# Softmax attention: normalising three of four head pairs later, from sums kept in DRAM

## The chip, the cores and the metric

The kernel runs on one core of a Trainium2 chip. Times are device microseconds of the program on that core. The engines are PE (TensorE, with its weight loads PEld), DVE (VectorE), ACT (ScalarE), POOL (GpSimd) and SP (SyncE, which here only issues transfers). Each engine takes its own instructions in program order, and waits on semaphores for the others.

## The reference

A two-layer trunk over 1040 tokens (16 learned ones and 1024) of width 1024. In each layer a group of gated-linear-attention heads (GLA) and a group of eight softmax heads with a forget bias (FoX) share one input projection; their normalised outputs go through one output projection, and a gated feed-forward block with a convolution of width 3 follows. The change is in the FoX heads:

```python
log_f = jax.nn.log_sigmoid(ff + b_forget[i])          # c = cumsum(log_f)
logits = einsum('bqhd,bkhd->bhqk', q_b * dh**-0.5, k) + c_q[..., None] - c_k[:, :, None, :]
logits = where(key_pos <= q_pos, logits, -inf)
o_fox = einsum('bhqk,bkhd->bqhd', softmax(logits), v)  # 8 heads of 64
o_fox = rms_norm(o_fox, fox_norm[i])                   # over the 64 of each head
h = h + concatenate([o_gla, o_fox], -1) @ w_out[i]
```

Because the norm follows, the softmax denominator d need not be divided out: with O the unnormalised sum over keys, `rms_norm(O/d) = O * rsqrt(mean(O*O) + EPS*d*d)`.

## The kernel before, in words

Activations are held with channels on partitions and tokens along the free side. Every large product is made in three passes of a split into a high and a low part (`mm<-xh,hi`, `mm<-xh,lo`, `mm<-xl,hi`, lines 257 to 259). Weights arrive as `raw`, and ACT or POOL and DVE split them (`hi`, `lo`, lines 224 and 226). The eight FoX heads are four pairs, p = 0 to 3, of two heads e = 0, 1. Tokens form nine tiles of 116 (the first 112), taken in five groups: (7,8), (5,6), (3,4), (1,2), (0).

`fox` walks over slots, one per pair, group, head and tile: 18 slots a pair, 72 in all. In a slot n a tile's scores are made (PE `S`, lines 713 and 714; DVE adds the bias row `cb` and takes the running minimum, line 716; ACT makes the exponential `P`, line 728). Two slots later P is transposed (PE `tr` line 749, ACT and DVE split it into `PT`, lines 373 and 374), three slots later the product with V follows (`av`, line 775). The fold (`fox_fold`) comes four slots after the last tile of head 1, and the store (`fox_store`) six. V holds high and low parts side by side, so that `av` has them in two partition halves, which ACT copies to `avs` (line 778). The fold transposes `avs` back to tokens on partitions (`fo`, line 788; four transposes for a two-tile group, two for the one-tile group), adds the halves (`ff`), squares and sums them along the free side (`fon`, `fv`), adds the squared denominator `fd`, takes the inverse root of the four numbers per token (`rsqrt`, lines 308 to 312: a logarithm and an exponential on ACT, three small operations on DVE) and multiplies (line 803). The store transposes the result again (line 814), ACT scales it into `fst` (line 821), and POOL's queue writes it to `mixd[4 + p]` in DRAM (line 822). For pair 3 the result goes into the operand of the output projection directly.

Between these steps `work.run` fills PE with other products, whose amount is planned by `plan(p)`: the next pair's projections, the GLA gate `gr` (evacuated by DVE, lines 673 to 684), and from slot 8 of pair 3 on (slot 62) the output projection (`wo`), whose operand is read back from `mixd` (`h<-mixd`, lines 1024 and 1032, on POOL's queue) and split into `mh` and `ml`. The Python order hands the steps to a list scheduler, which sets the final order on each engine; the scores have a higher priority. POOL also adds the causal mask to the next tile's columns of `cb` (line 893), and SP issues the loads of weights, of keys (`kA`, `kL`) and of the bias rows.

PSUM banks of one tag, `S`, serve the scores, the fold's and the store's transposes.

Of the kernel before, what the change touches and what calls it, by code (L numbers as in the profile page):

```python
# [168 lines left out]
class Kern:  # L169
    def __init__(self, ctx, tc, hT0, wm, wd, vec, wau, out):  # L170
# [26 lines left out]
        self.cd = dp.tile([8, T], F32, name="cd")  # L197
        self.later = []
# [554 lines left out]
    def fox_av(self, e, tiles, q, PT, avs, pp, part):  # L753
# [23 lines left out]
        if last < 4 * part + 4:  # L777
            nc.scalar.copy(avs[:, e, :width], av[:, :width])

# [27 lines left out]
    def fox_store(self, lyr, p, tiles, on, ap, pp, mix):  # L807
# [9 lines left out]
        if mix is not None:  # L817
            self.split(mix[0][:, c0:c0 + n], mix[1][:, c0:c0 + n], trf[:, :n], self.v(lyr, V_XN, p))
            return
        st = ap.tile([128, 2 * FT], F32, tag="fst", name="fst", bufs=1)  # L820
        nc.scalar.mul(st[:, :n], trf[:, :n], self.v(lyr, V_XN, p))
        nc.gpsimd.dma_start(self.mixd[4 + p][:, c0:c0 + n], st[:, :n])

    def fox(self, lyr, ap, pp, qs, plan, mix3):
# [9 lines left out]
        cbs, state, due = {}, {}, {}  # L834
# [9 lines left out]
        for n in range(len(steps) + 8):  # L844
# [7 lines left out]
            for kind in ('av0', 'T0'):  # L852
                run(n, kind)
            if n < len(steps):
# [12 lines left out]
                if e == 0 and ti == len(tiles) - 1:  # L867
                    state[p, g] = {"den": ap.tile([128, 2, 2], F32, tag="den", name="den", bufs=3)}
# [3 lines left out]
                with self.tc.high_priority(8):  # L872
                    Ps = self.fox_scores(e, i, qs[p], cbs[p][e], st["den"][:rows, ti, e:e + 1], ap, pp)
                if i:
                    self.fox_mask(cbs[p][e], i - 1)
                self.fox_schedule(lyr, at, n, p, e, ti, i, tiles, Ps, st, qs[p], ap, pp, mix3)
# [3 lines left out]
            run(n, "fold")  # L880
            for c in parts:
                run(n, "av" + c)
                run(n, "T" + c)
                work.run(fill_us / (1 + len(parts)))
        work.drain()
# [9 lines left out]
    def fox_schedule(self, lyr, at, n, p, e, ti, i, tiles, Ps, st, q, ap, pp, mix3):  # L895
# [18 lines left out]
        def av(ci):  # L914
            def f():
                if e == 0 and ci == 0:
                    one = len(tiles) == 1
                    st["avs"] = ap.tile([128, 2, FT if one else 2 * FT], F32, tag="av1" if one else "avs",
                                        name="avs", bufs=1)
                self.fox_av(e, tiles, q, PT, st["avs"], pp, ci)  # L920
# [5 lines left out]
        def store():  # L926
            self.fox_store(lyr, p, tiles, st["on"], ap, pp, mix3() if p == 3 else None)
        for ci in range(PT["nch"]):
            at(n + 3, f"av{ci}", av(ci))
        if e == 1:  # L930
            at(n + 4, "fold", fold)
            at(n + 6, "store", store)

# [6 lines left out]
    def attention(self, lyr, nm, hsrc, chunks, feed):  # L940
        tc, nc, s = self.tc, self.nc, self.slots
        with tc.tile_pool(name=f"aps{lyr}", bufs=2, space=PSUM, reuse_waits="tile") as pp2, \
# [64 lines left out]
            with tc.tile_pool(name=f"att{lyr}", bufs=2, reuse_waits="tile") as ap, \  # L1007
                    tc.tile_pool(name=f"lent{lyr}", bufs=1, reuse_waits="tile") as lp:
                s.lent = s.add(lp, 2, f"a{lyr}_")
                box = {}  # L1010
                KORD = (4, 5, 0, 1, 2, 3, 6)
# [929 lines left out]
```

## Time and profile before

| | |
|---|---|
| time, median of 3 runs | 2474.95 us (2473.05 to 2475.42) |
| profiled execution | 2476.73 us, its span 2474.8 us |
| granted PE clock, mean | 0.996 |
| PE busy | 2443.6 us (99%) |
| DVE busy | 1874.5 us (76%) |
| ACT busy | 1319.5 us (53%) |
| POOL busy | 383.1 us (15%) |

The profiled execution is 1.8 us above the median. Its span is the time from the first to the last instruction; 1.9 us lie around it. FoX takes from about 172 to 490 us in layer 0. In the rows of groups, the two numbers behind the bar are the busy time of all together and the mean ns of one; after the second bar stands the engine's idle time just before, and what ended most of it. In a row of the timeline the first number is the start, the second the duration.

### The profile page before, as it was taken

How to read it: one execution, taken by the hardware profiler on the slowest of the kernel's cores; microseconds unless marked ns; L12 is line 12 of the kernel's file. 1: busy time of each engine (PE TensorE's matmuls, PEld its weight loads, DVE VectorE, ACT ScalarE, POOL GpSimd, SP SyncE). 2: the span in 40 equal slices, each digit the busy share in tenths (PEclk: the TensorE clock that was granted, in tenths of full speed). 3: DMA queues.
4: the chain of work that ended last, by engine and by line, in shares of the span. 5: the costliest groups of instructions: out<-in, count | busy, mean ns of one | idle time of the engine just before them, and what ended most of it. 6: DMA issues, size and time to landing. Idle time of an engine off the chain costs nothing.

```text
span 2474.8 us, 47318 instructions
## 1 busy us (share of the span) xinstructions
PE 2443.6 (99%) x18286; PEld 2361.8 (95%) x18286; DVE 1874.5 (76%) x3769; ACT 1319.5 (53%) x2857; POOL 383.1 (15%) x565
## 2 busy tenths in 40 slices
PE   9999999999999999999999999999999999999998
PEld 8999999999999999999999999999999999997887
DVE  7656776869988888855866666777699888887667
ACT  7345666636555555642543456666465555556433
POOL 2023333210000000100220234331100000001002
PEclk9999999999999999999999999999999999999999
DMA  4232134433322224764312222243433212247722
GB/s 135 74 84 74 41 98 126 129 120 108 113 77 86 82 74 144 185 161 139 125 43 74 80 78 69 72 141 108 147 85 114 91 65 90 85 146 184 211 71 87
DMA packets 121824, 260.91 MB, mean 105 GB/s; under 512 B 15136, under 2 KB 36896, under 8 KB 121600
## 3 DMA queue, kind: packets, MB, share of 16 engines
q1 hardware_dynamic: 97440, 182.78, 23.9%
q0 software_dynamic: 22288, 72.81, 10.5%
q8 instruction: 143, 2.34, 0.4%
q10 hardware_dynamic: 1872, 2.31, 0.3%
q14 instruction: 81, 0.66, 0.1%
HBM read 177.26 MB, written 67.80 MB: 99 GB/s over the span
## 4 chain that ended last, share of the span: by engine, by line
PE 50%; issue 31%; DVE 11%; ACT 4%; DMA 2%; POOL 1%; SPq 0%; DVEq 0%; POOLq 0%; ACTq 0%
PE mm L257 8%; PE mm L259 7%; PE mm L258 7%; PE down L258 4%; PE down L257 4%; PE down L259 4%; PE av L775 3%; PE tr L749 2%; PE S L713 1%; DVE S L716 1%; PE wo L259 1%; PE wo L257 1%; PE wo L258 1%; PE S L714 1%; DVE x L1182 1%
## 5 line engine op out<-in xcount | busy, mean ns | idle before, releaser
L258 PE MATMUL up<-x,lo 128*128 128x260 f32 x2240 | 631.8, 282 | 0.8 <-DVE lo L1157 0.8
L259 PE MATMUL up<-x,hi 128*128 128x260 f32 x2240 | 631.8, 282 | 0.0
L257 PE MATMUL up<-x,hi 128*128 128x260 f32 x2240 | 631.7, 282 | 0.0
L258 PEld LDWEIGHTS up<-x,lo 128*128 128x128 f32 x2240 | 421.8, 188 | 1.3 <-DVE lo L1157 1.2
L257 PEld LDWEIGHTS up<-x,hi 128*128 128x128 f32 x2240 | 421.8, 188 | 0.2
L259 PEld LDWEIGHTS up<-x,hi 128*128 128x128 f32 x2240 | 421.9, 188 | 0.0
L1156 ACT CAST hi<-raw 128x512 fp32r<-128x512 f32 (+1 forms) x490 | 266.4, 553 | 208.2 <-PE up L259 89.2
L257 PE MATMUL mm<-xh,hi 128*128 128x348 f32 (+5 forms) x1056 | 361.2, 342 | 0.0
L1157 DVE TENSOR_TENSOR lo<-raw,hi 128x512 fp32r<-128x512 f32 (+1 forms) x490 | 288.1, 603 | 80.6 <-ACT hi L1156 80.1
L259 PE MATMUL mm<-xl,hi 128*128 128x348 f32 (+5 forms) x1056 | 340.5, 322 | 0.0
L258 PE MATMUL mm<-xh,lo 128*128 128x348 f32 (+5 forms) x1056 | 339.8, 322 | 0.0
L257 PEld LDWEIGHTS mm<-xh,hi 128*128 128x128 f32 x1056 | 200.3, 190 | 2.2 <-issue 1.4
L258 PEld LDWEIGHTS mm<-xh,lo 128*128 128x128 f32 x1056 | 200.5, 190 | 0.2
L259 PEld LDWEIGHTS mm<-xl,hi 128*128 128x128 f32 x1056 | 199.5, 189 | 0.1
L1138 DVE TENSOR_TENSOR raw<-raw,raw 128x512 f32<-128x512 f32 (+1 forms) x230 | 147.6, 652 | 28.1 <-DMA raw<-in_wd_dram 25.7
L728 ACT ACTIVATE P<-S,m 116x460 f32<-116x460 f32 (+2 forms) x224 | 125.0, 562 | 77.0 <-DVE m L716 74.1
L258 PE MATMUL down<-x,lo 128*128 128x260 f32 (+1 forms) x504 | 161.2, 320 | 0.5 <-DVE lo L1157 0.5
L259 PE MATMUL down<-x,hi 128*128 128x260 f32 (+1 forms) x504 | 161.1, 320 | 0.0
L257 PE MATMUL down<-x,hi 128*128 128x260 f32 (+1 forms) x504 | 161.0, 320 | 0.0
L224 ACT CAST hi<-raw 128x512 fp32r<-128x512 f32 (+2 forms) x152 | 87.4, 576 | 138.0 <-PE mm L259 53.7
L374 DVE TENSOR_TENSOR PT<-tr,PT 116x464 fp32r<-116x464 f32 (+3 forms) x240 | 123.2, 516 | 48.8 <-ACT PT L373 47.2
L1418 POOL DMA_DIRECT2D actd<-cv x44 | 23.6, 535 | 735.1 <-DVE cv L1417 735.1
(313 smaller groups left out, 5960.3 us busy)
## 6 DMA issues: line engine op xcount, KB each, us to landing
raw<-in_wm_dram SPq DMA_DIRECT2D x330, 256.0 KB, 3.1
raw<-in_wd_dram SPq DMA_DIRECT2D x48, 256.0 KB, 4.3
actd<-cv POOLq DMA_DIRECT2D x22, 520.0 KB, 3.0
actd<-cv POOLq DMA_DIRECT2D x22, 512.0 KB, 3.0
cb<-cd SPq DMA_DIRECT2D x16, 520.0 KB, 4.0
kA<-kA SPq DMA_DIRECT2D x24, 260.0 KB, 4.2
kL<-kL SPq DMA_DIRECT2D x24, 260.0 KB, 4.8
st<-actd SPq DMA_DIRECT2D x24, 260.0 KB, 3.5
```

The costliest lines, as they stand in the source:

```text
L224: nc.scalar.copy(hi[:, :n, :], raw[:, :n, :])
L257: nc.tensor.matmul(ps, wh, xh[:, c0:c0 + n], start=first, stop=False, skip_group_check=more)
L258: nc.tensor.matmul(ps, wl, xh[:, c0:c0 + n], start=False, stop=False, skip_group_check=more)
L259: nc.tensor.matmul(ps, wh, xl[:, c0:c0 + n], start=False, stop=last, skip_group_check=more)
L374: nc.vector.tensor_tensor(out=lo, in0=src, in1=hi.bitcast(F32), op=ALU.subtract)
L713: nc.tensor.matmul(S[:rows, :n], q["qA"][e][:, qs], q["kA"][e][:, c0:k1], start=True, stop=False)
L728: nc.scalar.activation(P[:rows, :n], S[:rows, :n], AF.Exp, scale=-1.0, bias=m[:rows, nch - 1:nch], accum_out=(den if nch == 1 else d3[:row ...
L749: nc.tensor.transpose(tr[:w, 3 - j, :rows], P[:rows, o:o + w], id_)
L775: nc.tensor.matmul(av[:, a:b], w.rearrange("p a b -> p (a b)"), x, start=(t == ts[0] and part == 0 and i == 0), stop=(t == last and i == 1))
L1138: nc.vector.tensor_tensor(out=q[out][:, :nk, :], in0=q[a][:, :nk, :], in1=q[b][:, :nk, :], op=op)
L1156: nc.scalar.copy(hi[:, :nk, :], src[:, :nk, :])
L1157: nc.vector.tensor_tensor(out=lo[:, :nk, :], in0=src[:, :nk, :], in1=hi[:, :nk, :].bitcast(F32), op=ALU.subtract)
```

## The change

Pair 3 stays as it was. For pairs 0 to 2 there is no fold and no store:

- `fox_av` copies one half of `av` with ACT, and DVE adds the other half: the sum O of a head, 64 rows by up to 232 columns. Behind head 1, POOL's queue stores the 128 rows of O to `mixd[4 + p]`, unnormalised. For groups 0 to 2 this store is handed out a slot later.
- The denominators of a pair gather in one tile (`denp`). `fox_den` squares and scales them after groups 2 and 4, PE transposes them, ACT copies them, and SP stores them as rows to DRAM (`dd`, `de`).
- Later (at 12, 10, 8, 6 and 6 slots behind a group's last tile) SP loads O back (`fO`, two buffers by turns), ACT squares it, and ACT and DVE split the square (`fsh`, `fsl`). A slot on, SP spreads the denominators over 64 partitions of each head (`fd`). Another slot on, PE sums the squares over each head's 64 rows with a block matrix of ones (`pair`, two matmuls of 232 columns, in a bank of tag `S`), DVE adds the denominators, the inverse root is taken on 128 rows by 232 columns (two ACT, three DVE operations), and DVE multiplies O in place. POOL's queue stores it to the same place of `mixd` in the slot after, for group 4 at once.

In slots of the pair, the norms fall at 17, 19, 21, 23 and 25: the last of a pair and the first eight of the next.

```diff
...
+            own, oth = slice(64 * e, 64 * e + 64), slice(64 - 64 * e, 128 - 64 * e)
+            nc.scalar.copy(avs[own, 0, :width], av[oth, :width])
+            nc.vector.tensor_tensor(out=avs[own, 1, :width], in0=av[own, :width], in1=avs[own, 0, :width], op=ALU.add)
+            if e:
+                return lambda: nc.gpsimd.dma_start(to[:, c0:c0 + width], avs[:, 1, :width])
...
-        st = ap.tile([128, 2 * FT], F32, tag="fst", name="fst", bufs=1)
-        nc.scalar.mul(st[:, :n], trf[:, :n], self.v(lyr, V_XN, p))
-        nc.gpsimd.dma_start(self.mixd[4 + p][:, c0:c0 + n], st[:, :n])
...
+    def fox_den(self, p, r, den, ap, pp):
+        nc.vector.scalar_tensor_tensor(out=d2..., in0=src, scalar=64.0 * EPS, in1=src, op0=ALU.mult, op1=ALU.mult)
+        nc.tensor.transpose(tr[:2 * n, 0, :FT], d2, self.ident[:FT, :FT])
+        nc.scalar.copy(row, tr[:2 * n, 0, :FT])
+        nc.sync.dma_start(self.dd[p][r][:], row)
+
+    def fox_load(self, p, g, tiles, st, ap):
+        st["O"] = O = ap.tile([128, 256], F32, tag=("fO", "fon")[g % 2], name="fO", bufs=1)[:, :n]
+        self.nc.sync.dma_start(O, self.mixd[4 + p][:, c0:c0 + n])
+
+    def fox_spread(self, p, g, tiles, st, ap):
+        for e in range(2):
+            self.nc.sync.dma_start(d2[64 * e:64 * e + 64], x[e:e + 1, a:a + n].to_broadcast([64, n]))
+
+    def fox_square(self, st, ap):
+        self.nc.scalar.activation(sq, O, AF.Square)
+        self.split(hi, lo, sq)
+
+    def fox_norm(self, lyr, p, tiles, st, ap, pp):
+        for i, x in enumerate(st["sq"]):
+            nc.tensor.matmul(ps, self.pair[:], x, start=i == 0, stop=i == 1)
+        nc.vector.tensor_tensor(out=v, in0=ps, in1=st["d2"], op=ALU.add)
+        self.rsqrt(y0, v, y0, a, scale=1.0 / 64)
+        nc.vector.scalar_tensor_tensor(out=O, in0=O, scalar=self.v(lyr, V_XN, p), in1=y0, op0=ALU.mult, op1=ALU.mult)
+        return lambda: nc.gpsimd.dma_start(self.mixd[4 + p][:, c0:c0 + n], O)
...
-        if e == 1:
+        if e == 1 and p == 3:
             at(n + 4, "fold", fold)
             at(n + 6, "store", store)
+        elif e == 1:
+            if g in (2, 4):
+                at(n + 2, "den", lambda: self.fox_den(p, int(g > 2), st["den"], ap, pp))
+            s0 = n + (12, 10, 8, 6, 6)[g]
+            at(s0, "load", lambda: self.fox_load(p, g, tiles, st, ap))
+            at(s0, "square", lambda: self.fox_square(st, ap))
+            at(s0 + 1, "spread", lambda: self.fox_spread(p, g, tiles, st, ap))
...
+            at(s0 + 2, "norm", norm)   # its store at s0 + 3, for group 4 at once
```

The program's order on the engines moves at three places that matter below. Line numbers of the changed kernel differ: its scores are 714, 715 (PE) and 717 (DVE), its transposes 750, its split 375, its products 258 to 260, `av` 776, the root 311 to 313.

The first is the crossing from pair 1 to pair 2 in layer 0, around the third slot of pair 2. On PE before, with the fold and three score chunks of head 1 (460, 464 and 116 columns):

```order
L788 MATMUL fo<-ident,avs 116x128 x4
L775 MATMUL av<-PT_4457,V_2331 128x112
L713 MATMUL S<-kA_3500,qA_3498 116x460
L775 MATMUL av<-PT_4457,V_2331 128x112
L714 MATMUL S<-kL_3502,qA_3498 116x460
L749 MATMUL tr<-ident,P 116x116
L713 MATMUL S<-kA_3500,qA_3498 116x464
L749 MATMUL tr<-ident,P 116x116
L714 MATMUL S<-kL_3502,qA_3498 116x464
L749 MATMUL tr<-ident,P 116x116 x2
L713 MATMUL S<-kA_3500,qA_3498 116x116
L714 MATMUL S<-kL_3502,qA_3498 116x116
```

And on PE after:

```order
L873 MATMUL fs<-fsh,pair 128x232
L873 MATMUL fs<-fsl,pair 128x232
L776 MATMUL av<-PT_4446,V_2343 128x112 x2
L714 MATMUL S<-kA_3479,qA_3477 116x460
L715 MATMUL S<-kL_3481,qA_3477 116x460
L750 MATMUL tr<-ident,P 116x116 x4
L714 MATMUL S<-kA_3479,qA_3477 116x464
L715 MATMUL S<-kL_3481,qA_3477 116x464
L258 MATMUL mm<-xh_150,hi 128x348
L259 MATMUL mm<-xh_150,lo 128x348
L260 MATMUL mm<-xl_151,hi 128x348
```

The two sums of squares (`fs`) stand where the four fold transposes stood, and the chunk of 116 columns stands 16 rows behind the one of 464, after planned products.

On DVE at the same place, before (`ff`, `fv`, `fa`: the fold of the preceding group):

```order
L792 TENSOR_TENSOR ff<-fo,ff 116x256
L716 ISA S,m<-S,cb 116x460
L716 ISA m 116x1
L798 TENSOR_REDUCE fv<-fon 116x4
L716 ISA S,m<-S,cb,m 116x464
L716 ISA m 116x1
L799 TENSOR_TENSOR fv<-fv,fd 116x4
L374 TENSOR_TENSOR PT_4523<-tr,PT_4523 116x4x116
L310 SCALAR_TENSOR_TENSOR fa<-fy 116x4
L716 ISA S,m<-S,cb,m 116x116
L716 ISA m 116x1
L311 TENSOR_TENSOR fa<-fa,fv 116x4
```

and after (`fw`: the root's operands):

```order
L876 TENSOR_TENSOR fw<-fs,fd_4340 128x232
L375 TENSOR_TENSOR PT_4513<-tr,PT_4513 116x4x116
L375 TENSOR_TENSOR PT_4514<-tr,PT_4514 116x4x116
L311 SCALAR_TENSOR_TENSOR fw<-fw 128x232
L717 ISA S,m<-S,cb,m 116x116
L717 ISA m 116x1
L312 TENSOR_TENSOR fw<-fw 128x232
L313 SCALAR_TENSOR_TENSOR fw<-fw 128x232
L375 TENSOR_TENSOR PT_4513<-tr,PT_4513 116x4x116
L878 SCALAR_TENSOR_TENSOR fO<-fO,vec,fw 128x232
L375 TENSOR_TENSOR fsl<-fsq,fsh 128x232
```

The root's three operations and the product, 4 columns wide or 128 before, are 232 wide, and stand between the splits of transposed scores and ahead of the next scores.

The second place is DVE in pair 3 of layer 0, where the output projection begins; `ml` is the low part of its operand. Before:

```order
L732 TENSOR_REDUCE den<-d_6159 116x1
L792 TENSOR_TENSOR ff<-fo,ff 116x256
L374 TENSOR_TENSOR PT_6069<-tr,PT_6069 116x2x116
L673 TENSOR_TENSOR gx<-mm,r 128x344
L798 TENSOR_REDUCE fv<-fon 116x4
L676 TENSOR_SCALAR ge<-gx 128x344
L799 TENSOR_TENSOR fv<-fv,fd 116x4
L680 TENSOR_TENSOR gog<-gx,gog 128x344
L374 TENSOR_TENSOR ml_6239<-h_5881,mh_6238 128x256
L374 TENSOR_TENSOR ml_6241<-h_5882,mh_6240 128x256
```

After:

```order
L733 TENSOR_REDUCE den<-d_6171 116x1
L375 TENSOR_TENSOR ml_6263<-h_5868,mh_6262 128x256
L375 TENSOR_TENSOR PT_6081<-tr,PT_6081 116x2x116
L375 TENSOR_TENSOR ml_6259<-h_5866,mh_6258 128x384
L375 TENSOR_TENSOR ml_6265<-h_5869,mh_6264 128x256
L682 SCALAR_TENSOR_TENSOR ge<-ge,gy 128x348
L375 TENSOR_TENSOR ml_6267<-h_5870,mh_6266 128x256
L683 SCALAR_TENSOR_TENSOR gy<-ge,gy 128x348
L375 TENSOR_TENSOR ml_6269<-h_5871,mh_6268 128x256
L685 SCALAR_TENSOR_TENSOR h_5868<-gy,gog 128x348
L876 TENSOR_TENSOR fw<-fs,fd_6068 128x112
```

The low parts of the 256-column chunk now stand ahead of pair 3's fold and of the last gate evacuation, and the norm of pair 2's last group stands behind them.

The third is POOL's queue in pair 3 of layer 0. Before:

```order
L1024 DMA h_5879<-mixd_93 128x1040
L822 DMA mixd_97<-fst 128x112
L1032 DMA h_5883<-mixd_97 128x400
L893 TENSOR_TENSOR cb<-cb,mask 116x116
L1050 DMA h_5877<-in_hT_dram 128x256
```

After:

```order
L879 DMA mixd_97<-fO 128x232
L1122 DMA h_5871<-mixd_97 128x384
L958 TENSOR_TENSOR cb<-cb,mask 116x116
L687 DMA mixd_93<-gog 128x348
L1114 DMA h_5867<-mixd_93 128x1040
L958 TENSOR_TENSOR cb<-cb,mask 116x116
```

Before, one of the three loads of `mixd[6]` stood directly behind a store of it; after, all three do (one is shown), each with a mask behind.

More of the change, by code (lines that the diff above doesn't have):

```diff
@@ L880, in fox @@
             run(n, "fold")
+            run(n, "norm")
             for c in parts:
@@ L1010, in attention @@
                 box = {}
+                self.pair = ap.tile([128, 128], F32R, tag="pair", name="pair", bufs=1)
+                for e in range(2):
+                    h, z = slice(64 * e, 64 * e + 64), slice(64 - 64 * e, 128 - 64 * e)
+                    nc.scalar.copy(self.pair[h, h], self.ones[h, h])
+                    nc.scalar.mul(self.pair[h, z], self.ones[h, z], 0.0)
                 KORD = (4, 5, 0, 1, 2, 3, 6)
```

76 lines of the change are left out of this document (61 added, 15 removed).

## The prediction

> **What bounds the kernel now.** I read the page from its first two parts down, then the chain, and then the windows, waits and timeline of the stretch that the change touches.
>
> ```profile
> PE 2443.6 (99%) x18286; PEld 2361.8 (95%) x18286; DVE 1874.5 (76%) x3769; ACT 1319.5 (53%) x2857; POOL 383.1 (15%) x565
> PE 50%; issue 31%; DVE 11%; ACT 4%; DMA 2%; POOL 1%; SPq 0%; DVEq 0%; POOLq 0%; ACTq 0%
> ```
>
> PE is busy for 2443.6 of 2474.8 us, and the chain that ended last runs mostly through PE and its issue. So a PE instruction taken out is worth its pace, unless another engine then holds PE up. The averages can't say where that happens; the softmax stretch (172 to 490 us in layer 0, its like in layer 1) has to be read in windows. The columns are PE, PE loads, DVE, ACT and POOL busy, granted PE clock, DMA share, GB/s.
>
> ```profile
> 248.00:254.00 6.00, 6.00 (x41) 5.64 (x39) 4.60 (x17) 4.97 (x18) 1.60 (x3) 1.00 0.01 3
> 254.00:260.00 6.00, 5.86 (x40) 4.98 (x38) 5.89 (x24) 4.53 (x17) 0.98 (x2) 1.00 0.19 59
> 260.00:266.00 6.00, 6.00 (x45) 5.65 (x44) 5.79 (x14) 5.28 (x14) 3.22 (x5) 1.00 0.18 46
> 266.00:272.00 6.00, 6.00 (x47) 5.93 (x46) 5.87 (x21) 4.34 (x14) 1.76 (x3) 1.00 0.38 126
> 272.00:278.00 6.00, 6.00 (x45) 5.93 (x45) 3.84 (x12) 3.59 (x10) 3.07 (x5) 1.00 0.21 69
> 446.00:452.00 6.00, 5.93 (x45) 5.63 (x42) 6.00 (x18) 5.86 (x18) 2.08 (x4) 1.00 0.32 88
> 452.00:458.00 6.00, 4.32 (x24) 4.32 (x25) 6.00 (x20) 6.00 (x17) 1.09 (x2) 0.72 0.38 111
> PE mm L259 <- DVE ml L374: 1.7, 1, 1.7
> ```
>
> The first five are the crossing from pair 0 to pair 1: PE is full, but from 254 to 272 DVE is busy for 17.55 of 18 us, and PE waits 0.14. The next two are pair 3, where the output projection begins: DVE is full for 12 us and PE loses 1.75. The last row is the only wait above 1 us that PE has in the whole stretch. So PE bounds, with DVE close behind it at the crossings and level with it in pair 3.
>
> **PE work taken out.** PE is pipelined, so its price is the distance between starts. The first row is the first score matmul of pair 1, and the one at 408.83 that of pair 3: 81.7 us a pair, 4.5 us for each of its 18 slots.
>
> ```profile
> 245.48 0.42 PE L713 MATMUL S<-kA,qA 128*116 128x460 f32 x1
> 301.30 0.32 PE L259 MATMUL mm<-xl,hi 128*128 128x348 f32 x1
> 301.46 0.33 PE L257 MATMUL mm<-xh,hi 128*128 128x348 f32 x1
> 302.90 0.60 PE L788 MATMUL fo<-ident,avs 128*116 128x128 f32 x4
> 303.25 0.94 PE L775 MATMUL av<-PT,V 116*128 116x256 f32 x6
> 408.83 0.42 PE L713 MATMUL S<-kA,qA 128*116 128x460 f32 x1
> 451.30 0.38 PE L749 MATMUL tr<-ident,P 116*116 116x116 f32 x2
> 451.45 0.36 PE L257 MATMUL mm<-mh,hi 128*128 128x256 f32 x1
> 451.65 0.28 PE L258 MATMUL mm<-mh,lo 128*128 128x256 f32 x1
> 453.68 0.38 PE L259 MATMUL mm<-ml,hi 128*128 128x256 f32 x1 [1.75 <-DVE ml L374]
> 453.90 0.28 PE L257 MATMUL mm<-mh,hi 128*128 128x256 f32 x1
> 454.02 0.28 PE L258 MATMUL mm<-mh,lo 128*128 128x256 f32 x1
> 454.89 0.41 PE L258 MATMUL mm<-mh,lo 128*128 128x256 f32 x1
> 455.11 0.41 PE L259 MATMUL mm<-ml,hi 128*128 128x256 f32 x1
> 457.54 0.41 PE L259 MATMUL mm<-ml,hi 128*128 128x256 f32 x1
> ```
>
> A 348-column matmul takes 0.16 us, a 256-column one 0.12 (453.90 to 454.02), so one of 232 columns 0.11. Four fold transposes take 0.35, two plain ones 0.15, and the matmul behind transposes takes 0.20 (451.45 to 451.65) where its like takes 0.12: 0.08 more. A two-tile group loses four fold transposes (0.43) and two back transposes (0.23), and gains two 232-column matmuls (0.22): -0.44. A one-tile group loses about half and gains 0.11: -0.2. Pairs 0 to 2 of two layers hold 24 and 6 groups: -10.6 and -1.2. The 12 denominator transposes, at 0.08 and the 0.08 behind each, add 1.9. PE total: **-9.9 us**. Bounds: -11.8 if the twelve hide, -7.5 if the 48 added matmuls of two-tile groups cost 0.16 like those of 348 columns.
>
> **DVE work put in.**
>
> ```profile
> L792 DVE TENSOR_TENSOR ff<-fo,ff 116x256 f32<-116x256 f32 x15 | 6.3, 421 | 5.4 <-ACT ff L791 5.0
> L798 DVE TENSOR_REDUCE fv<-fon 116x4 f32<-116x256 f32 x15 | 6.3, 420 | 3.7 <-ACT fon L794 3.7
> L799 DVE TENSOR_TENSOR fv<-fv,fd 116x4 f32<-116x4 f32 x15 | 3.7, 248 | 0.2
> L311 DVE TENSOR_TENSOR fa<-fa,fv 116x4 f32<-116x4 f32 x15 | 2.9, 193 | 0.4
> L803 DVE TENSOR_TENSOR fon<-ff,fy 116x128 f32<-116x128 f32 x30 | 7.4, 286 | 0.3
> L374 DVE TENSOR_TENSOR PT<-tr,PT 116x232 fp32r<-116x232 f32 x15 | 5.9, 393 | 2.9 <-ACT PT L373 2.7
> ```
>
> Before, a two-tile group costs DVE 0.42 + 0.42 + 0.25 + four 4-wide operations of at most 0.19 + two of 0.29: 2.4 us. After, it is eight operations of 232 columns (two half adds, the square's low part, the sum with the denominators, three of the inverse root, the product), each like the 393 ns row: 3.1 us. I see no reason for the 64-partition adds to be cheaper than that; if they cost the 0.29 of the 128-column row it is 2.9. So +0.75 a group, and more where it counts: the norms move from all over the pair to slots 17 to 25, that is the crossing. Pricing by such rows what the order has on DVE in slots 17 to 24, I get 29.2 us before and 35.2 after, against 39.5 us of PE (crossing slots are longer than the mean). On average it fits. But slot 20 alone goes from 5.2 to 8.1, and the 254 to 272 stretch has 0.45 us to spare. Some 2.5 us then spill into the slots behind, where 272 to 278 has 2.2 free.
>
> What it costs PE lies between 0 (the S, transpose and product banks let PE run ahead) and those 2.5 per crossing. The two full stretches of the windows give rates: PE lost 0.14 in 18 us in the one and 1.75 in 12 in the other. If the full stretch grows by the 6 us, that is 0.05 to 0.9; I take 0.4, just under the middle, since the 1.75 came from the load of the mix and not from scores. Four crossings (pairs 0-1 and 1-2, two layers): **+1.6 us** (0 to 10).
>
> **Pair 3.** The norms of pair 2 now fall into its slots up to 61, beside its own folds, which stay. By the same count DVE has 58.4 us of work there before and 63.4 after, in 62.8 us of PE, so it is full throughout. The 1.75 wait at 453.68 is for the low part of the loaded mix; behind it the granted clock falls to 0.72 (the 452 window), and matmuls come every 0.22 us (454.89 to 455.11) instead of 0.12, still at 457.54 by the length of its row. Some 3.2 us at about half speed are 1.5 us more, so one such event costs 3.3. After, the low parts of that chunk stand ahead of the fold and the gate's evacuation instead of behind them, which would shorten this wait; but the norm, the fold and the next score reductions stand behind the low parts then, and the wait may move to those. Bounds per layer: -3.3 (the event goes) to +5.0 (all added DVE time shows). I take half another event, 1.6, nearest to the row that exists: **+3.2 us** for two layers.
>
> [...]
>
> **ACT, POOL, SP, DMA.**
>
> ```profile
> L1032 POOL DMA_DIRECT2D h<-mixd x3 | 1.6, 544 | 8.0 <-issue 4.2 <-DMA mixd<-fst 2.3 <-PE S L714 1.5
> mixd<-fst POOLq DMA_DIRECT2D x12, 116.0 KB, 3.5
> SPq L864 <- DVE fv L799: 9.6, 3, 3.4
> 403.04 2.65 SPq L864 DMA_DIRECT2D cb<-cd  x2
> ```
>
> ACT loses a fold copy and the scaled copy out, and gains the square's cast and a logarithm and an exponential of 232 columns instead of 4; about level, and ACT is 53% busy: nothing. POOL issues 30 more stores at 0.54 like that load, 16 us on an engine that is 15% busy: nothing, but its masks for the next tile stand behind them. Where a load of the mix stands right behind a store of it, the load waits for the landing (4.2 us as L1032 did) and the mask behind both. There are three such loads per layer instead of one; a slot of 4.5 us covers 4.2, and PE has no wait above 1 us there. I cost it at nothing; uncovered, it is up to 0.5 us each, 3 us. SP issues 100 more transfers. Each reload waits for the sum's landing (3.5 us for 116 KB, under a slot), with weights and bias rows behind it. The bias rows of the next pair are the tightest: issued from 403.04 for pair 3's first score at 408.83, after waiting for DVE themselves. I cost that at nothing too; uncovered, a late landing of up to 3.5 us at six pair changes.
>
> **Sum.** -9.9 + 1.6 + 3.2 = -5.1 us, against the profiled execution's own 2476.73: 2471.6. That execution stands 1.8 above the median of the runs, 2474.95, so I predict **2469.8 us**. A change under 0.2% (4.95 us) can hardly be told from none here; the forecast sits just past it.
>
> **Rivals.**
>
> *The whole PE saving comes through.* PE waits 0.14 us in 18 where DVE is 97% busy, which speaks for deep enough banks; the full stretch of pair 3 speaks against. With no stall added: 2474.95 - 9.9 = 2465.0 us.
>
> *DVE and POOL hold each other up, and the gain is cancelled.*
>
> ```profile
> 262.85 1.45 DVE L682 SCALAR_TENSOR_TENSOR gy<-ge,gy 128x348 f32<-128x348 f32 x1
> 262.64 1.28 POOL L226 TENSOR_TENSOR lo<-raw,hi 128x512 fp32r<-128x512 f32 x1
> 264.33 0.52 DVE L684 SCALAR_TENSOR_TENSOR gog<-gy,gog 128x348 f32<-128x348 f32 x1
> L226 POOL TENSOR_TENSOR lo<-raw,hi 128x512 fp32r<-128x512 f32 x22 | 28.6, 1305 | 31.9 <-ACT hi L224 31.8
> L893 POOL TENSOR_TENSOR cb<-cb,mask 116x116 f32<-116x116 f32 x62 | 28.3, 456 | 97.4 <-DVE m L716 79.3 <-DVE fa L310 4.4 <-DMA cb<-cd 4.0
> ```
>
> A DVE product of 348 columns took 1.45 us beside a POOL subtraction and its like 0.52 after it. The new DVE operations that read two stored tiles number five a group, 150 in all; POOL's subtractions and masks run for some 18% of the stretch (28.6 and 28.3 in 318 us), so about 27 meet one and lose some half of it, 0.45 on average: 12 us of DVE. If 45% of that falls where DVE is full (18 us of a 39.5 us crossing), PE loses 5.4 on top of the forecast: 2475.2 us, no change. [...]
>
> *Slower: DVE becomes the bound at the crossings.* The spill of 2.5 us shows in full at four crossings and pair 3 pays a whole event more in each layer: -9.9 + 10 + 6.6 = +6.7, 2481.6 us. For it speaks the 8.1 us of DVE in slot 20; against it, that PE passed 18 nearly full DVE microseconds with 0.14 lost. It decides from 9.9 / 6 = 1.65 us per crossing; from 2.5 the kernel is slower by more than 0.2%.
>
> **How the numbers follow.** Forecast (2467 to 2473) 0.40, full saving 0.18, cancelled 0.19, slower 0.23. A little over half of the forecast's own range, 0.23, lies below 2470.0; with the full saving that makes faster 0.41. The rest of it and the cancelled case make same 0.36, and slower has 0.23. The range runs from 2462, the full saving and its -11.8 bound with an execution's scatter, to 2482, the slower case's middle; about 0.1 is left out above and less below.
>
> **What would show it.** Right: PE matmul time of the fold and back transposes gone but pair 3's, pair periods down from 81.6 by 1 to 1.8 us, DVE near full from slot 19 to 22, and a wait of PE on a low part in pair 3 with the clock below 1 behind it. Wrong: PE idle of a microsecond or more per crossing released by DVE (the slower case), DVE operations of 1 us beside POOL's subtractions (the cancelled one), no stall at all (full saving), or a first score of a pair waiting for the bias rows, which I cost at nothing.

## The result and the profile after

The changed kernel takes 2509.94 us (median of 4 runs, 2507.54 to 2513.01), against 2474.0 before (4 runs, 2471.51 to 2475.42): a ratio of 1.0145, 95% interval 1.0133 to 1.0157. It is slower by 36 us, outside the range of 2462 to 2482, where a gain was forecast (2469.8). The profiled span grew from 2474.8 to 2505.8 us, by 31: the profiled execution of before stands 1.8 above its median, that of the changed kernel 2.4 below.

The page after, its busy times and its chain:

```profile
PE 2442.2 (97%) x18196; PEld 2348.5 (94%) x18196; DVE 1901.8 (76%) x3757; ACT 1330.3 (53%) x2847; POOL 402.1 (16%) x601
PE 60%; issue 17%; DVE 14%; ACT 6%; DMA 3%; POOL 1%; SPq 0%; DVEq 0%; ACTq 0%; POOLq 0%
```

DVE is busy only 27 us more and ACT 11. PE's share fell from 99 to 97%, which is 32 us more of standing (63.6 against 31.2 us). What it waited for, over the whole span (total, times, longest):

```profile
PE S L714 <- ACT P L729: 12.2, 16, 1.2
PE tr L836 <- ACT P L729: 9.5, 6, 1.7
PE tr L750 <- DVE PT L375: 6.8, 9, 1.4
PE mm L259 <- DVE wl L227: 3.4, 3, 1.7
PE fs L873 <- ACT P L729: 3.3, 2, 1.7
PE fs L873 <- ACT fsh L374: 3.3, 6, 1.0
```

The 3.5 us wait for the low part of the mix is gone, and in its place there are many small ones. Most are waits for a PSUM bank of the scores, which the exponential (`P`, line 729) gives back: at scores (714), at the denominators' transposes (836), at the sums of squares (873).

The crossing from pair 0 to 1, which starts at 242.01 here, in windows (columns as before):

```profile
242.00:248.00 6.00, 4.55 (x32) 4.13 (x30) 4.79 (x15) 2.73 (x8) 1.96 (x4) 1.00 0.45 149
248.00:254.00 6.00, 5.54 (x33) 4.90 (x34) 4.27 (x17) 5.30 (x22) 0.43 (x1) 1.00 0.07 20
254.00:260.00 6.00, 6.00 (x42) 5.48 (x41) 5.69 (x16) 3.70 (x10) 1.69 (x3) 1.00 0.19 59
260.00:266.00 6.00, 5.11 (x35) 4.62 (x34) 5.10 (x14) 5.71 (x17) 3.84 (x4) 1.00 0.44 123
266.00:272.00 6.00, 4.85 (x38) 4.55 (x36) 5.47 (x17) 3.51 (x9) 1.55 (x3) 1.00 0.42 138
272.00:278.00 6.00, 5.68 (x37) 5.02 (x38) 4.77 (x15) 5.13 (x16) 2.14 (x4) 1.00 0.13 41
```

PE lost 4.3 us in these 36. DVE has room by its sum in all of them, 30.1 of 36. So it isn't full; it is late. The first of the waits, in the rows of DVE, ACT and PE in order of time (put together from the three engines' timelines of the changed kernel):

```profile
242.87 0.40 DVE L311 SCALAR_TENSOR_TENSOR fw<-fw 128x232 f32<-128x232 f32 x1 [0.89 <-ACT fw L310]
243.00 0.22 PE L714 MATMUL S<-kA,qA 128*116 128x116 f32 x1
244.79 0.45 DVE L878 SCALAR_TENSOR_TENSOR fO<-fO,vec,fw 128x232 f32<-128x232 f32 x1
245.16 0.64 DVE L717 CUSTOM_DVE_ANT_0 S<-S,cb 116x460 f32<-116x460 f32 x1
247.45 0.64 ACT L729 ACTIVATE P<-S,m 116x460 f32<-116x460 f32 x1 [1.73 <-DVE m L717]
248.23 0.26 PE L836 MATMUL tr<-ident,fdp 116*6 116x116 f32 x1 [1.69 <-ACT P L729]
```

PE has made all three score chunks by 243.3, and they hold the three banks. DVE works off the norm of the first group first (311 to 878), and reduces the first chunk only at 245.16. The exponential comes at 247.45, and the next PE instruction that needs such a bank, here the transposes of the denominators, stands for 1.69 us with the planned products behind it.

The distance between the first score matmuls of slots gives the loss by place. In the table, "crossing" is slots 18 to 25 (the first eight of a following pair) of pairs 1 and 2, "rest" their other ten, "pair 3" the last pair up to its last slot; means over the two layers, in us more than before. The kernels behind the first row are the experiments of the next section:

| kernel | pair 0 | each crossing | each rest | pair 3 | all |
|---|---|---|---|---|---|
| changed | -2.0 | +4.8 | +0.5 | +7.5 | +31.9 |
| without the later half (no_norm) | -1.8 | -0.2 | -1.9 | +2.1 | -7.7 |
| its transfers alone (dma_only) | -2.4 | +0.9 | -1.9 | +4.3 | 0.0 |
| transfers and square (square_only) | -2.2 | +2.9 | -1.9 | +4.2 | +7.9 |
| transfers, root, product (no_square) | -2.2 | +3.7 | -1.9 | +6.0 | +14.7 |
| all but the sums on PE (no_fs) | -2.0 | +6.2 | -1.5 | +5.6 | +26.1 |
| later norms (norm_late) | -2.5 | +2.5 | +2.6 | +9.1 | +33.5 |
| five additions at the norms (tied_norm) | -1.9 | +3.0 | -1.8 | +4.7 | +10.5 |
| the same at the folds (tied_fold) | -1.6 | +2.3 | -1.9 | +4.2 | +7.0 |
| before, without fold (before_nofold) | -1.6 | -1.0 | -2.0 | -1.8 | -18.5 |

"All" is 2 x pair 0 + 4 crossings + 4 rests + 2 x pair 3, that is both layers. Pair 0 shows what was gained, the crossings and pair 3 where it was lost. Of pair 3's 7.5 us, 6.5 fall in its first eight slots, which are the third crossing of the layer. In the rests the changed kernel has lost again what the kernels without the sums on PE keep (+0.5 against -1.5 to -1.9).

### The profile page after: what moved, and what is told of

The parts are those of the page before. It is cut to its first block, busy times and chain, and to the rows that moved or that the text cites. A ratio compares the mean times of both kernels' runs of the same rounds, so it can differ in the third digit from the quotient of the medians.

```text
span 2505.8 us, 47612 instructions
## 1 busy us (share of the span) xinstructions
PE 2442.2 (97%) x18196; PEld 2348.5 (94%) x18196; DVE 1901.8 (76%) x3757; ACT 1330.3 (53%) x2847; POOL 402.1 (16%) x601
## 4 chain that ended last, share of the span: by engine, by line
PE 60%; issue 17%; DVE 14%; ACT 6%; DMA 3%; POOL 1%; SPq 0%; DVEq 0%; ACTq 0%; POOLq 0%
PE mm L258 7%; PE mm L259 7%; PE mm L260 7%; PE up L260 5%; PE up L259 5%; PE up L258 5%; PE down L258 4%; PE down L259 4%; PE down L260 4%; PE av L776 2%; PE tr L750 2%; DVE S L717 1%; ACT P L729 1%; PE S L714 1%; DVE x L1272 1%
## 5 line engine op out<-in xcount | busy, mean ns | idle before, releaser
L374 ACT CAST PT<-tr 116x464 fp32r<-116x464 f32 (+3 forms) x240 | 106.1, 449 | 85.8 <-PE tr L750 81.7
```

The costliest lines, as they stand in the source:

```text
L374: nc.scalar.copy(hi, src)
```

## The experiments

Theories: order (the norm's chain stands ahead of the score reductions on DVE), time (the DVE and ACT work is too much where it stands), bank (the score banks have too many users), and, further on, shared tiles, chain, transfers and place. All edits are to the changed kernel unless said otherwise, and are shortened. The runs of before that were made beside the experiments have medians of 2472.96 to 2474.94, so the difference of two experiments is uncertain by 1 to 2 us.

### Bank: other PSUM banks

```diff
-        tr = pp.tile([128, 4, 128], F32, tag="S", name="tr")     # fox_den
+        tr = pp.tile([128, 4, 128], F32, tag="tr", name="tr")
```

> The denominators' transposes take a PSUM bank of the tag that the transposed scores use, instead of one of the three that scores use. Order theory (the norm's chain stands ahead of the score reductions on DVE, so the scores' banks come free late, and PE, in order, waits at whatever needs one next): the wait of 9.5 us at the denominators' transposes goes, but about half comes back at the next scores or transposes; 2503 to 2507 us, against the changed kernel's 2509.94. Bank theory (a fourth user of three banks is the cause): 10 us or more go with the wait, 2490 to 2500. DVE-time theory (the added DVE work is simply too much at the crossings): no change, 2508 to 2511.

2515.76 us (2513.72 to 2520.55): slower still, which none of the three theories expected. The wait at the denominators' transposes went, PE waited for transposed scores instead (9.2 us at `av` against 1.7), and the crossings cost 8.0 each instead of 4.8.

```diff
-        ps = pp.tile([128, 512], F32, tag="S", name="fs")[:, :n]
+        ps = pp.tile([128, 512], F32, tag="mm", name="fs")[:, :n]
```

> The sums of squares take one of the two PSUM banks of the planned products instead of one of the three of the scores. Bank theory: waits at scores go, 2490 to 2500 us. DVE-time theory: the sum's bank is held until DVE reads it, now in the way of the products, 2508 to 2520.

2510.42 us, no change: the products now wait 10.0 us for the sums' bank. In both runs the waits moved to another place. The bank is where PE notices the lateness, not its cause.

### The later half left out

```diff
-            at(s0, "load", ...)   and "square", "spread", "norm"
```

> Leaves out the later half for pairs 0 to 2: no reload, no square, no spread, no norm, no second store; the sums and the denominators are still stored, and the output projection reads the unnormalised sums. Order theory and DVE-time theory: nearly all of the loss goes, and the PE work of the sums of squares as well: 2458 to 2472 us. Bank theory: the denominators' transposes still wait, some 10 us: 2472 to 2485. If the loss sat in the first half (half adds that wait for ACT, the stores), 2490 or more.

2464.38 us (2463.31 to 2465.9), ratio to before 0.9962 (0.9948 to 0.9977). The later half costs 45.6 us, more than the whole loss of 36; the first half alone, half adds and stores, is 8.9 us faster than before. By the prediction's prices it should have been 15.9 faster (17.8 for the fold and the store, less 1.9 for the denominators' transposes), so some 7 us of the gain are missing here already. The table puts them at pair 3 (+2.1 against -1.8 without any fold) and at the crossings (-0.2 against -1.0); no run separates what takes them. PE's waits for a score bank then come to

```profile
PE S L714 <- ACT P L729: 3.7, 10, 0.6
```

with none at the denominators' transposes, though these are still there.

### Order: scores first, and no ACT in the chain

```diff
-                with self.tc.high_priority(8):
+                with self.tc.high_priority(40):
```

> Only the scheduler's priority of the scores is raised from 8 to 40 steps, so that at a crossing the score reductions stand ahead of the norm's chain on DVE; the work is the same. Order theory: the bank waits at the crossings go; some of it comes back since the order changes elsewhere too: 2475 to 2495 us. DVE-time theory: as much DVE work in the same slots, 2505 to 2515. Bank theory: the denominators' transposes still take a score bank, 2500 to 2512.

2516.21 us, 6 us slower, above all three expectations. On DVE the score reductions do stand ahead of the norm now, and the waits change their names:

```profile
PE S L714 <- DVE fw L876: 18.7, 14, 2.5
PE fs L873 <- ACT fsh L374: 11.1, 6, 2.4
```

The sum of squares now holds its bank until DVE comes to it, and PE stands at the sums for squares that are late. Whichever goes first on DVE, PE's fixed order meets the one that goes second.

```diff
-        self.rsqrt(y0, v, y0, a, scale=1.0 / 64)
+        # the same three DVE operations on v and a, without ACT's logarithm and exponential
```

> The inverse root's logarithm and exponential on ACT are left out for pairs 0 to 2; the three DVE operations stay, at the same width, on other operands (these heads come out as zero). DVE then has the same work, but no wait for ACT inside the chain. Order theory: the chain shortens by the two ACT operations and four semaphore hops, some 1.5 us at each of 30 norms, of which a third or so reached PE: 2490 to 2500 us. DVE-time theory: 2506 to 2511. Bank theory: about as DVE time, 2505 or more.

2510.08 us, no change. The wait for ACT inside the chain (0.89 in the rows above) is not the cause. The order theory falls with both.

### Time: parts of the norm left out

```diff
-        for i, x in enumerate(st["sq"]):
-            nc.tensor.matmul(ps, self.pair[:], x, start=i == 0, stop=i == 1)
```

> The two PE matmuls that sum the squares are left out for pairs 0 to 2; the reload, the square, its split, the spread and every DVE and ACT operation of the norm stay, the sum with the denominators reading the spread denominators twice. PE then never waits for the norm, and no score bank holds its sums. PE-side theory (PE in its fixed order waits for the squares, and the sums hold one of three score banks until DVE reads them): the loss goes, 2465 to 2480 us. DVE-time theory (the norm's DVE work stands before score reductions in short slots, and the scores' banks come free late): the waits at scores and denominators stay, 2495 to 2508; 6 us of it is the PE work left out.

2504.72 us: 5.2 less, for 6.0 us of PE work by the prediction's price. PE loses about as much when it has nothing to do with the norm at all. What stalls it is DVE and ACT being late for the scores and the transposed scores (10.2 us at the denominators' transposes, 13.5 at `av`).

```diff
-        self.rsqrt(y0, v, y0, a, scale=1.0 / 64)
...
+        nc.vector.scalar_tensor_tensor(out=O, in0=O, scalar=0.0, in1=v, op0=ALU.mult, op1=ALU.mult)   # the product, on v
```

> The inverse root is left out for pairs 0 to 2 (three DVE operations of 232 columns and two of ACT in each norm; those heads come out as zero); squares, sums, spread, the sum with the denominators and the product in place stay. DVE-time theory: three of the norm's six DVE operations go, 1.2 of 2.4 us, so about half of the loss of 36: 2485 to 2498 us. PE-side theory: the sums and their bank stay, the bank is read as late as before: 2503 to 2511.

2501.7 us, 8.2 less: between the two expectations, and half or less of what the time theory expected (12 to 25).

```diff
+        n = st["O"].shape[1] // 2; O = st["O"][:, :n]       # fox_square, and alike in fox_norm
```

> The changed kernel with squares, sums, root and product on half of each group's columns (the other half is stored unnormalised); transfers whole. The number of instructions and of waits stays, their time nearly halves. DVE-time theory: half of the 36 us over the transfers alone go: 2488 to 2494. Chain theory: the hops stay and only part of the durations goes: 2499 to 2507.

2502.31 us, 7.6 less, 3 of it PE work: inside the second expectation, that of the chain theory. But an operation of half the width is far from half as long, so it is a weak test against the time theory. The group rows of the square's low part, of the changed kernel

```profile
L375 DVE TENSOR_TENSOR fsl<-fsq,fsh 128x232 fp32r<-128x232 f32 x12 | 4.7, 396 | 2.1 <-ACT fsh L374 2.0
```

and at half the width:

```profile
L375 DVE TENSOR_TENSOR fsl<-fsq,fsh 128x116 fp32r<-128x116 f32 x12 | 3.5, 292 | 3.3 <-ACT fsh L374 3.3
```

### Place: the norms later, the squares later

```diff
-            s0 = n + (12, 10, 8, 6, 6)[g]
+            s0 = n + (12, 10, 8, 6, 6)[g] + (9, 7, 0, 0)[p]
```

> The norms of pairs 0 and 1 stand 9 and 7 slots later, so in slots 8 to 16 (6 to 14) of the next pair instead of 17 of the own to 7 of the next; pair 2's stay. Place theory (the crossing is where DVE has no room): four of the six crossings lose their cost of 4.7 us each and the norms cost little where they now stand: 2488 to 2496 us. If the cost belongs to the norm's operations wherever they stand (each stalls PE by about 1 us): 2503 to 2512.

2510.02 us, no change. The crossing from pair 0 to 1 is then nearly free (+0.7 and +0.6 in the two layers), but the norms cost where they now stand: the rests go from +0.5 to +2.6, and the next crossing, in which those of pair 1 begin, still costs +4.7 and +3.9.

```diff
-            at(s0, "square", lambda: self.fox_square(st, ap))
+            at(s0 + 1, "square", lambda: self.fox_square(st, ap))
```

> The square and its split are handed out one slot later, at the end of the slot before the norm, when the preceding norm has left the work tiles that both share. Shared-tile theory (the square's tiles are the norm's and the gate's, so ACT, in order, stands waiting at the square until DVE has finished the preceding norm, and exponentials and casts behind it come late): 10 to 20 us less than the changed kernel's 2509.94, 2490 to 2500. Time theory (it is the norm's DVE and ACT time in all, wherever it stands): 2505 to 2515.

2519.34 us, 9 us worse, above both expectations: PE stood 19.2 us at the sums for late squares. So the two slots of lead are needed, and the run says little of the shared tiles. In the changed kernel ACT stands 19.8 us at the square and its cast until DVE has left a shared tile. They are not the main cause, since without squares (no_square, below) most of the loss at the crossings stays; what separate tiles would bring was not run.

### The parts alone

```diff
-            at(s0, "square", ...)         # dma_only and no_square
-        ...body of fox_norm, but its store  # dma_only and square_only
-        ...the two matmuls                  # no_square
```

> Of the later half only the transfers stay, for pairs 0 to 2: the reload, the spread, and the second store, of the sums as they were loaded. If the transfers on SP and POOL hold nothing up: as without the later half, 2463 to 2468 us. If reloads, spreads and stores delay weights, keys or bias rows: 2475 or more.

2473.63 us (2469.44 to 2480.34; ratio 0.9998, 0.9988 to 1.0008), between the two expectations: the transfers alone take back the 9 us that the first half gained. The largest stall, in the timelines of POOL, ACT and PE:

```profile
410.16 0.49 POOL L950 TENSOR_TENSOR cb<-cb,mask 116x116 f32<-116x116 f32 x1 [3.67 <-DMA cb<-cd]
414.23 0.25 ACT L782 COPY avs<-av 64x112 f32<-64x112 f32 x1 [3.83 <-DMA mixd<-avs]
415.78 0.46 PE L776 MATMUL av<-PT,V 112*128 112x112 f32 x1 [2.62 <-ACT PT L374]
```

The sum's tile has one buffer. ACT stands until the store of the last sum has landed, with the casts of the transposed scores behind it. The store was issued only at 410.60: it stood in POOL's queue behind a mask, which waited 3.67 us for the bias rows (`cb<-cd`). In the changed kernel ACT has no such wait; so the parts don't simply add up.

> Of the later half the transfers, the square and its split stay for pairs 0 to 2; the sums on PE, the root and the product are left out. Time theory: a sixth of DVE's and half of ACT's part, 2470 to 2478 us. Shared-tile theory: the tiles are then shared with the gate alone, 2466 to 2475. Neither is told from the other here; it prices the square by itself.

2481.6 us, 8.0 over the transfers alone, for two ACT operations and one of DVE per group: more than either theory expected.

> Leaves out the square, its split and its sums for pairs 0 to 2 (two ACT operations, one of DVE, two matmuls per group); the reload, the spread, the root and the product stay. Shared-tile theory: most of the loss goes, 2470 to 2485 us. Time theory: a sixth of the norm's DVE time and half of its ACT time go, and 6 us of PE: 2492 to 2502.

2491.79 us, 18.2 over the transfers alone. Together the two parts would make 26.2; both at once, without the sums on PE (no_fs), make 31.1. No part is the cause; each adds its share.

### What the old fold cost, and what DVE time alone costs

The kernel before, without fold and normed store for pairs 0 to 2:

```diff
-        if e == 1:
+        if e == 1 and p < 3:
+            at(n + 4, "fold", lambda: self.nc.gpsimd.dma_start(self.mixd[4 + p][...], st["avs"][:, 0, :w]))
+        elif e == 1:
```

> The kernel before, with the fold and the normed store of pairs 0 to 2 left out (a store of one unnormalised half stands in for the store). Its PE time by my prices is 17.8 us. If the fold's DVE and ACT time were hidden and only its PE time on the path: 2455 to 2459 us. If its DVE and ACT time cost like the norm's: 2430 to 2445. If the fold was hidden even in part of its PE time: 2462 to 2468.

2454.97 us, against 2472.96 of before beside it: 18.0 us (15 to 22 by the interval of the ratio, 0.9912 to 0.9939), which is the 17.8 of its PE work. The fold's DVE and ACT time was hidden, as far as this can tell.

In no_norm, five additions in place of each norm:

```diff
+                for _ in range(5):
+                    self.nc.vector.tensor_tensor(out=X, in0=one, in1=one, op=ALU.add)
```

> As without the later half, but at each norm's place five DVE additions of the norm's width are put in that wait for nothing, that nobody waits for, and that feed nothing. DVE-time theory: they cost what the root and the product cost over the transfers alone, 18 us: 2478 to 2485. Chain theory (it is the steps that wait for one another across engines): no change from 2464.38: 2462 to 2468.

2483.65 us, the expected number for the wrong reason. With operands ready from the start, the scheduler had put all of them into pair 0, which lost 5.8 us a layer, and the crossings none (-0.1). A lump of them in DVE's timeline, eight in a row:

```profile
202.85 3.46 DVE L1011 TENSOR_TENSOR fO<-ones 128x232 f32<-128x232 f32 x8
```

So the operand was taken from the slot before:

```diff
+                one = self.dprev.to_broadcast([k, len(tiles) * cols])   # denominators of the slot before
```

> As without the later half (2464.38 us), with five DVE additions of the group's width at each norm's slot, held there by an operand of the slot before; nobody waits for them, and ACT, PE and the queues get nothing. DVE-time theory: what root and product cost over the transfers alone, 18 us, at the crossings: 2478 to 2486. Chain theory: a wait for another engine or for a tile is needed to hold PE up: 2464 to 2470.

2486.47 us, 22.1 more than without the later half. Nobody waits for these additions, they wait for nothing but their operand, and they use no bank, no ACT, no transfer. They cost 3.2 us at each crossing (+3.0 against -0.2) and hardly anything in the rests (-1.76 against -1.87).

> The same additions at the slots where the old fold stood, four behind a group's last tile, spread over the pair. Place theory: the old fold's DVE time cost nothing there, so neither do these: 2464 to 2470 us. DVE-time theory without regard to place: as at the norms' slots, 2478 to 2486.

2480.47 us, 16.1 more: the number of the theory without regard to place. But by the trace three of the five groups' additions, 15 of 25, stand in the crossing here too. They cost 2.5 us there, and the ten in the rests nothing (-1.89). With the norms' slots it was 20 additions for 3.2 us: in both runs some 0.16 us of PE for each addition of 0.39 us that falls in a crossing. Place, then, means the crossing, not the slot offset.

Some of the additions meet POOL. Two rows of DVE and POOL, of tied_norm:

```profile
262.78 1.41 DVE L1014 TENSOR_TENSOR fO<-denp 116x232 f32<-116x232 f32 x1
262.45 1.49 POOL L227 TENSOR_TENSOR lo<-raw,hi 128x512 fp32r<-128x512 f32 x1 [1.54 <-ACT hi L225]
```

Sixteen of the 150 additions of tied_norm took 0.7 to 1.4 us instead of 0.39, 13 us of DVE more in all; in tied_fold ten, 8 us more. So "DVE time alone" includes what additions lose beside POOL, 1.02 us in the one shown.

The stretch from 254 to 272 us of the kernel before, of no_norm, tied_norm and tied_fold, one fence each:

```profile
254.00:272.00 18.00, 17.86 (x126) 16.57 (x125) 17.55 (x57) 14.15 (x44) 5.97 (x9) 1.00 0.25 77
```

```profile
254.00:272.00 18.00, 17.67 (x123) 16.68 (x122) 16.40 (x41) 12.93 (x37) 6.01 (x9) 1.00 0.26 81
```

```profile
254.00:272.00 18.00, 15.42 (x106) 14.21 (x105) 17.55 (x48) 11.88 (x32) 5.90 (x8) 1.00 0.22 64
```

```profile
254.00:272.00 18.00, 15.89 (x108) 14.53 (x108) 17.38 (x48) 12.43 (x34) 5.14 (x8) 1.00 0.23 67
```

DVE is busy for 17.55 us in the first and in the third, and PE loses 0.14 in the one and 2.58 in the other. The busy share of DVE in a window does not tell what more work will cost: the window is as full, and the work that no longer fits stands behind it. The crossing starts some 3 us earlier in the third, too. Over the whole crossing from pair 0 to 1, of before, of tied_norm and of the changed kernel:

```profile
245.48:285.64 40.16, 40.02 (x278) 38.01 (x278) 32.77 (x103) 29.28 (x90) 14.58 (x22) 1.00 0.20 63
242.33:285.03 42.70, 39.62 (x267) 36.74 (x267) 37.97 (x109) 26.96 (x79) 14.72 (x22) 1.00 0.20 61
242.01:287.02 45.01, 40.73 (x274) 37.60 (x274) 37.45 (x112) 32.22 (x93) 16.22 (x25) 1.00 0.26 81
```

DVE is busy 5 us more in the second and the third than in the first. It is never full over the crossing, and PE loses 3.1 and 4.3 us.

### A cheaper fold

The kernel before with the halves added ahead of the fold, for all pairs, and one transpose per tile:

```diff
-            nc.scalar.copy(avs[:, e, :width], av[:, :width])
+            nc.scalar.copy(avs[own, 0, :width], av[oth, :width])
+            nc.vector.tensor_tensor(out=avs[own, 1, :width], in0=av[own, :width], in1=avs[own, 0, :width], op=ALU.add)
```

> The kernel before, for all four pairs, with the halves added before the fold as the changed kernel does it (an ACT copy of half the rows, a DVE addition): the fold then takes one transpose per tile instead of two and no addition behind them. PE saves 0.2 us in a two-tile group, 8 us or less in all; DVE has 0.35 us more per group. If only PE time counts: 2466 to 2469 us. If DVE time displaces PE at a third: 2469 to 2474. If the order on the engines shifts badly, as in the changed kernel: 2476 or more.

2481.63 us, ratio 1.0037 (1.0024 to 1.0049). PE does less and the kernel is slower. That 0.35 us of DVE more in each group cost more than they saved is argued, not shown: the order on the engines changed as well, and the run doesn't separate the two. No version that was run and computes everything beats the kernel before.

## Why the prediction was wrong

**PE's prices were right.** Leaving the old fold out gave 18.0 us where the prices made it 17.8, and leaving the new sums out 5.2 where they made it 6.0. In no_norm the rests fell by 1.9 us each. But the -9.9 did not come through even without the norm: no_norm shows 8.9 of its 15.9.

**DVE's durations were right.** 392 to 396 ns for most 232-column operations, 450 for the product, against the 393 that was taken.

**The crossing term failed: 0.4 us each, measured 4.8, with what PE saved there already taken off.** The step was "the two full stretches of the windows give rates": it took PE's idle share beside a nearly full DVE and multiplied it by the time added. That share says what the work in place costs, and it was nearly nothing; it doesn't say what other work costs there. The premise of the full DVE failed too: in the changed kernel DVE is busy 37.5 of the crossing's 45.0 us, and PE stands because single reductions come late. The upper bound failed as well: 2.5 us, the DVE time that spills, where tied_norm alone shows 3.2 and the whole change 4.8. The rows from 242 to 248 show how one late reduction is passed on, to the exponential, the bank and the PE instructions behind; that the casts of the transposed scores pay for it again is read from the waits and was not priced.

**The pair 3 term failed: 1.6 a layer, measured 7.5** (from the first slot of pair 3 to the last). The part of it that was read from the order was right: the wait for the low part of the mix went. But pair 3 opens with a crossing as well, the third of its layer, and 6.5 of the 7.5 fall there; the term had no price for it. Late in it stand two waits at the sums, 0.99 at 449.54 and 1.64 at 462.78, and behind it one for a weight, 1.69 at 473.22. The windows around the second one:

```profile
458.00:464.00 6.00, 4.36 (x29) 4.06 (x29) 6.00 (x19) 6.00 (x18) 2.61 (x5) 0.95 0.37 109
464.00:470.00 6.00, 6.00 (x42) 5.90 (x41) 5.45 (x16) 5.30 (x16) 2.05 (x4) 0.77 0.38 116
```

The granted clock fell again, to 0.77 in the second window, after a wait of 1.64.

**What was costed at nothing.** Bias rows and reloads: right for the changed kernel, no wait of PE for them above 0.2 us. The 16 us of POOL stores and the sum's single buffer: not nothing by themselves, as dma_only shows (9 us over no_norm), though hidden behind the other lateness here. And the bias rows do reach PE there, by a way that the prediction did not look at: mask, store, ACT.

**The rivals.** The slower one named the place and the direction, and began at 2.5 us a crossing and 3.3 in pair 3; it was half as large as what came. The cancelled one was small. In the timelines of DVE and POOL of the changed kernel:

```profile
288.42 1.19 DVE L311 SCALAR_TENSOR_TENSOR fw<-fw 128x112 f32<-128x112 f32 x1 [0.90 <-ACT fw L310]
288.20 1.29 POOL L227 TENSOR_TENSOR lo<-raw,hi 128x512 fp32r<-128x512 f32 x1 [1.06 <-ACT hi L225]
```

The DVE operation ended 0.12 us behind POOL's, and took 0.92 more than its like (0.27). Of the root's 30 first operations (line 311) eight took so much longer, each beside a POOL operation that ended 0.12 to 0.26 us before it: four of the 24 on two-tile groups (0.93 or 0.94 us instead of 0.39) and four of the six on one-tile groups (1.19 to 1.21). Of all the norm's other operations only two did: some 6.3 us of DVE in all, not 12.

**What stays open.** The additions cost some 0.4 us of PE for each us of DVE in a crossing, and the fold's like amount of DVE time, with three of five folds in a crossing as well, cost none. One reading is that the crossing had room for just the fold: without it DVE is busy 30.6 us there (before_nofold), with it 32.8; no_norm stands at 32.4 already, by its half adds, and tied_fold at 36.0, tied_norm at 38.0. That is argued from sums, and what DVE loses beside POOL is not taken out of it. Nor were the shares of ACT, of the shared tiles and of the chain in the remaining half of the 45.6 us separated.

## What to carry to other kernels

A busy share of an engine, and what its neighbour loses beside it, price the work that is there and not the work that is added. Where one engine feeds another through few buffers in a fixed order, as DVE does here for PE through three banks, put the planned amount of idle instructions at the place and run that; hold them there with an operand, since a scheduler moves free work elsewhere. Taking work off the bounding engine only pays if the engine that gets it has room at that place, and not on the mean.

## What the runs showed of the hardware

The clock fell after waits of PE of 1.64 us (0.77 in the window behind it) and 1.75 us (0.72 before the change), both in pair 3, and stayed at 1.00 in the windows around one of 1.69 at the crossing. So the length of a wait alone does not tell whether the clock falls.

The traces of the two kernels show it in finer pieces. In both the granted clock changes only on a grid of pieces of 3.413 us, to 1.00 or 0.50. Two such pieces of the kernel before, around its wait of 1.75, and two of the changed kernel, the first with a wait of 1.70:

```profile
451.08:454.49 3.41, 1.66 (x15) 1.46 (x14) 3.41 (x13) 3.41 (x12) 0.00 (x0) 1.00 0.25 77
454.49:457.90 3.41, 3.41 (x19) 3.41 (x18) 3.41 (x11) 3.41 (x9) 1.09 (x2) 0.50 0.48 127
```

```profile
333.69:337.10 3.41, 1.71 (x11) 1.55 (x11) 2.60 (x10) 2.45 (x10) 0.42 (x1) 1.00 0.21 70
337.10:340.51 3.41, 3.19 (x22) 2.72 (x20) 2.42 (x10) 2.77 (x11) 0.43 (x1) 1.00 0.00 1
```

PE stood for 1.75 us within the first piece of the kernel before, and the next one ran at half clock; it stood for 1.70 within that of the changed kernel, and the clock stayed. Of the 1442 pieces at full clock in the two traces, without the first 10 us and the end of each, five were followed by one at 0.50; PE stood for 1.36 to 1.82 us in them. It stood for 1.15 to 1.70 us in 18 others, behind which the clock stayed at 1.00, and for less than 1.13 in the rest. What decides between the two was not shown.
